# All engines in program order, weight parts ahead of the matmuls, gathers on the sync queue

## The chip, the cores and the metric

The kernel runs on one core of one Trainium2 chip. The metric is the device time in microseconds of one execution. Engines are written as in the profile: PE (TensorE, matmuls), DVE (VectorE), ACT (ScalarE), POOL (GpSimd), SP (SyncE, whose queue issues most DMAs).

## The reference

Two layers over 256 positions of width 2048, all in float32. Cut to what matters:

```python
for l in range(DEPTH):                      # 2
    h = rms_norm(x, mix_norm[l])
    proj = h @ w_in[l]                      # -> q 1024 | k 256 | v 256 | u,v 2048 | gates 4096
    q, k = apply_rope(rms_norm(q, ...)), apply_rope(rms_norm(k, ...))
    branch_a = sliding_window_attention(q, k, v, sinks[l]) @ w_attn_branch[l]   # 16 heads, window 128
    branch_b = chunked_sgu(gelu(uv), w_spatial[l], ...) @ w_sgu_branch[l]
    gates = sigmoid(gate_logits)
    merged = gates[..., :D_MODEL] * branch_a + gates[..., D_MODEL:] * branch_b
    x = x + merged @ w_out[l]
    h2 = rms_norm(x, ffn_norm[l])
    x = x + (silu(h2 @ w_gate[l]) * (h2 @ w_up[l])) @ w_down[l]                 # D_FF 5632
```

## The kernel before

**Products.** A float32 weight is split into two numbers of a shorter type, a high part `whi` (ACT copies `raw` to it, line 198) and a low part `wlo` = `raw` - `whi` (DVE, line 199). Activations are split the same way, into `uh` and `ul`. A product is three matmuls into one accumulator bank of PSUM: `whi` with `uh`, `wlo` with `uh`, `whi` with `ul` (lines 267 to 269).

**Jobs, steps, parts.** Every projection is a list of jobs, each for 1024 columns of a weight matrix (`add_job`), with four accumulator banks: two column halves c, two blocks of 128 positions t. A job runs over *units*, 512 rows of the weight with the matching transposed slice of the activations. A unit takes four *whole* steps of 12 matmuls. Each step uses one *part* of weights, 256 rows by 512 columns. In the jobs of w_out, w_gate, w_up and w_down the first unit (`M_OUT`, `M_FFN`, `M_DOWN` = 1) is done with seven products of half blocks in place of eight (`PRODUCTS`, in the order 11, t1, t2, 22, t3, 21, t4). These are seven *short* steps of 6 matmuls. Four of their weight parts are differences of others (DVE, line 193), their activations are sums too (`sums`, `sh`, `sl`), and between them ACT and DVE copy and add accumulator banks (`acc`, `p5`, `u2`, lines 294 to 317). When the last step of a column half c is done, `done(c, ...)` reads its banks: `hid`, `gate`, `xs` and so on. The half c = 0 ends one step before c = 1.

**Weights.** `raw` has four buffers of 1 MB, loaded by SP. `whi` and `wlo` have five buffers each (`W_SPLIT`).

**Transposing activations.** A finished chunk of 512 columns becomes a unit by `transposed`. Either PE transposes it (`on_pe`, line 406, eight small matmuls into `pt`), or `gathered` does. There DVE transposes 32 by 32 blocks into `blk` (line 359), of which there is one buffer, and sixteen DMAs of 32 KB, issued by POOL (line 364), carry the blocks to their places in `tt`. `done` in `transposed` splits the result `G_WAIT` = 8 steps later.

**Order.** Only PE follows the program's order. On the other engines a scheduler that estimates times places the instructions, guided by marks in the code: `tc.high_priority()` around what reads a bank, and `tc.issue_after(...)` for delayed work. Work is delayed by `after(n, fn)`, which runs `fn` n steps later, at a `tick`; a short step counts half.

The lines that set how far ahead weights are made:

```python
def next(self):
    self.load(parts[self.at][0][0] + W_LOAD)
    self.split(self.at + W_SPLIT)
    self.at += 1
```

[...]

Of the kernel before, what the change touches and what calls it, by code (L numbers as in the profile page):

```python
# [14 lines left out]
P = 128  # L15
# [17 lines left out]
W_LOAD = 4  # L33
W_SPLIT = 5
N_WARM = 8
N_BIG = 23
AHEAD = 2
G_WAIT = 8
K_TURN = 7
Q_TURN = 7  # L40
Q_FIRST = 17
Q_STEP = 4
LOAD_BY = (1, 1, 2, 2)
# [7 lines left out]
def hybrid_trunk(ctx: ExitStack, tc: tile.TileContext, x, mix_norm, w_in, q_norm, k_norm, sinks,  # L51
# [7 lines left out]
    wraw = ctx.enter_context(tc.tile_pool(name="wraw", bufs=W_LOAD))  # L59
    wsp = ctx.enter_context(tc.tile_pool(name="wsp", bufs=W_SPLIT))  # L60
# [4 lines left out]
    ps_tr = ctx.enter_context(tc.tile_pool(name="ps_tr", bufs=2, space=bass.MemoryType.PSUM))  # L65
    ps_at = ctx.enter_context(tc.tile_pool(name="ps_at", bufs=2, space=bass.MemoryType.PSUM))
# [38 lines left out]
    def add_job(cols, units=None, m=0):  # L105
# [5 lines left out]
        for i, name in enumerate(PRODUCTS if m else ()):  # L111
            for n, u in enumerate(job.units[:m]):
                a, b = held[u]
                v = {"11": (a, 0), "12": (a, 1), "21": (b, 0), "22": (b, 1)}
                src, total = {"11": ("11", None), "22": ("22", None), "21": ("21", None),
                              "t1": ("11", ("12", "11")), "t2": ("11", ("22", "11")),
                              "t3": ("12", ("22", "12")), "t4": ("11", ("21", "11"))}[name]
                parts.append((v[src], total and (v[total[0]], v[total[1]])))
                job.steps.append((name, u, n == m - 1))
        for u in job.units[m:]:  # L120
            if not job.pair:
                a = load_of(job, u)
                for h in range(2):
                    parts.append(((a, h), None))
                    job.steps.append(("whole", u, (h, 0)))
            else:
                for h in range(2):
                    a = load_of(job, u, h)
                    for c in range(2):
                        parts.append(((a, c), None))  # L130
                        job.steps.append(("whole", u, (h, c)))

    for l in range(DEPTH):
        wl = w_in[l]
        add_job([wl[:, O_KV:O_KV + CW]])
        for o in (0, O_V, O_U, O_GATE, O_GATE + CW2):
# [17 lines left out]

    class Stream:

        def __init__(self):
            self.raws, self.parts, self.lows = [], [], []
            self.at = 0

        def anchor(self):
            return self.lows[min(len(self.lows), self.at + AHEAD) - 1]

        def load(self, upto):
            while len(self.raws) < min(upto, len(loads)):
                job, srcs = loads[len(self.raws)]
                raw = wraw.tile([P, 2 * CW2], F32, tag="raw", name=nm("raw"))
                if not job.pair:
                    v = raw.rearrange("p (h k n) -> p h k n", h=2, n=CW)
                    views = [v[:, h] for h in range(2)]  # L170
                    for h in range(2):
                        src = srcs[0][:, 2 * h:2 * h + 2]
                        for k in range(2) if not self.raws else (None,):
                            ks = slice(0, 2) if k is None else slice(k, k + 1)
                            self.loaded = nc.sync.dma_start(views[h][:, ks], src[:, ks])
                else:
                    v = raw.rearrange("p (k c n) -> p k c n", c=2, n=CW)
                    views = [v[:, :, c] for c in range(2)]
                    if job.wide:
                        self.loaded = nc.sync.dma_start(raw.rearrange("p (k n) -> p k n", n=CW2), srcs[0])  # L180
                    else:
                        for c in range(2):
                            self.loaded = nc.sync.dma_start(views[c], srcs[c])
                self.raws.append(views)

        def split(self, upto):
            while len(self.parts) < min(upto, len(parts)):
                (i, j), total = parts[len(self.parts)]
                self.load(i + 1)
                raw = self.raws[i][j]  # L190
                if total is not None:
                    (ia, ja), (ib, jb) = total
                    nc.vector.tensor_tensor(out=raw, in0=self.raws[ia][ja], in1=self.raws[ib][jb], op=ALU.subtract)  # L193
                hi = wsp.tile([P, 2, CW], F32R, tag="hi", name=nm("whi"))
                lo = wsp.tile([P, 2, CW], F32R, tag="lo", name=nm("wlo"))
                one = len(self.parts) < 2
                for k in ([slice(0, 1), slice(1, 2)] if one else [slice(0, 2)]):
                    nc.scalar.activation(hi[:, k, :], raw[:, k, :], AF.Copy)  # L198
                    last = nc.vector.tensor_tensor(out=lo[:, k, :], in0=raw[:, k, :], in1=hi[:, k, :].bitcast(F32),  # L199
                                                   op=ALU.subtract)  # L200
                self.parts.append((hi, lo))
                self.lows.append(last)
# [11 lines left out]
    slot_no = [0]  # L214

# [3 lines left out]
    def tick(n=1):  # L219
        slot_no[0] += n  # L220
        due = [s for s in steps if s[0] <= slot_no[0]]
        steps[:] = [s for s in steps if s[0] > slot_no[0]]
        for _, fn in sorted(due, key=lambda s: s[0]):
            with tc.issue_after(stream.anchor().ins):
                fn()
# [3 lines left out]
    for c in range(NCH):  # L229
# [3 lines left out]
        stream.load(LOAD_BY[c])  # L233
# [26 lines left out]
    banks = [0, 1, 2, 3]  # L260
# [10 lines left out]
    def run(units, done):  # L271
# [3 lines left out]
        own = [acc(b) for b in (banks if job.pair else banks[:2])]  # L275
        if job.m:
            a, e, x, y = own
            ps = [[x, y], [e, a]]
            banks[:] = [banks[2], banks[3], banks[1], banks[0]]
            into = {"11": a, "t1": e, "t2": a, "22": e, "t3": a, "21": x, "t4": y}  # L280
            begun = {id(x), id(y)}
            held = {}
        elif job.pair:
            ps = [own[:2], own[2:]]
            begun = set()
        else:
            ps = [own]
            banks[:] = banks[2:] + banks[:2]
            begun = set()
# [6 lines left out]
        for n, (name, u, at) in enumerate(job.steps):  # L296
            hi, lo = stream.next()
            unit = units[u]
            if name != "whole":
# [5 lines left out]
                if at:  # L305
                    with tc.high_priority():
                        if name == "11":
                            nc.scalar.activation(x, a, AF.Copy)  # L308
                        elif name == "t1":
                            kept("p5", e)  # L310
                        elif name == "t2":
                            kept("u2", a)
                        elif name == "22":
                            nc.vector.tensor_tensor(out=e, in0=e, in1=held["u2"], op=ALU.add)  # L314
                        elif name == "t3":
                            nc.scalar.activation(y, a, AF.Copy)
                            nc.vector.tensor_tensor(out=a, in0=a, in1=held["p5"], op=ALU.add)
# [12 lines left out]
            if left[c] == 0:  # L330
                with tc.high_priority():
                    done(c, ps[c])
# [599 lines left out]
```

## Time and profile before

| What | Value |
|---|---|
| Median of 2 runs | 2598.59 us (2595.84 to 2601.33) |
| The profiled execution | 2600.37 us, its span 2598.7 us |
| DVE making `wlo`, 1012 instructions | 1220.3 us |
| ACT making `whi`, 1012 instructions | 1057.9 us |
| POOL issuing gathers for `tt`, 416 DMAs | 239.9 us |
| Weights moved, HBM read | 475.27 MB, 184 GB/s over the span |

The span runs from the first instruction of the program to its last. Busy time of an engine is the time in which at least one of its instructions ran; an idle time is put down to the instruction on another engine that ended it (`<-`). A row of the timeline gives the start, the duration, and in brackets the idle time before it. Consecutive matmuls overlap, so their pace is read from their starts and not from their durations.

### The profile page before, as it was taken

The page shows a single profiled execution, that of the slowest core. Times are in us where ns is not written, and L with a number is a line of the kernel's source. Part 1 is how long each engine was busy: PE and PEld are TensorE (multiplying, and loading weights), DVE is VectorE, ACT ScalarE, POOL GpSimd, SP SyncE. Part 2 cuts the span into 40 slices and gives each one's busy share as a digit, 9 for nine tenths or more (in the row PEclk, how much of TensorE's full clock was granted, in tenths as well). Part 3 has the DMA queues.
Part 4 walks back from the last instruction along what each step waited for, and adds up shares of the span by engine and source line. Part 5 has one row for each costly group of instructions (what it writes and reads, how often), then busy time and mean ns, then how long its engine had stood idle before and what let it go on. Part 6 is the DMA issues. An engine that isn't in the chain of part 4 may idle for free.

```text
span 2598.7 us, 29795 instructions
## 1 busy us (share of the span) xinstructions
PE 2515.0 (97%) x11230; PEld 2066.4 (80%) x11230; DVE 1838.5 (71%) x2109; ACT 1332.1 (51%) x1650; POOL 337.8 (13%) x559
## 2 busy tenths in 40 slices
PE   9999999999999999999989999999999999999999
PEld 7778888777788777878777788887777887788787
DVE  6785546786877687677867855467868676877786
ACT  5454444464554555455644544444645455554554
POOL 3312102030200020001123121020202000200010
PEclk9999999999999999999999999999999999999999
DMA  8645666555464655555666446564654646465654
GB/s 291 209 136 162 188 194 209 162 189 200 162 218 171 226 179 192 197 204 193 205 200 206 150 155 194 194 208 149 215 189 164 216 171 225 164 213 176 220 177 162
DMA packets 150608, 496.11 MB, mean 191 GB/s; under 512 B 16384, under 2 KB 19040, under 8 KB 150464
## 3 DMA queue, kind: packets, MB, share of 16 engines
q1 hardware_dynamic: 133408, 476.87, 54.3%
q0 software_dynamic: 16736, 17.06, 2.7%
q8 instruction: 88, 1.44, 0.2%
q14 instruction: 56, 0.46, 0.1%
q10 hardware_dynamic: 320, 0.27, 0.0%
HBM read 475.27 MB, written 2.10 MB: 184 GB/s over the span
## 4 chain that ended last, share of the span: by engine, by line
PE 89%; DVE 6%; ACT 3%; issue 1%; DMA 1%; POOL 0%; DVEq 0%; SPq 0%; ACTq 0%; POOLq 0%
PE acc L267 29%; PE acc L268 29%; PE acc L269 29%; DVE wlo L199 2%; ACT whi L198 1%; PE pt L406 1%; DVE raw L193 1%; PE po L698 1%; DVE ul L381 1%; DVE hid L878 0%; PE ppt L688 0%; ACT junk L447 0%; DMA tt<-blk 0%; DVE v L749 0%; PE psc L660 0%
## 5 line engine op out<-in xcount | busy, mean ns | idle before, releaser
L199 DVE TENSOR_TENSOR wlo<-raw,whi 128x1024 fp32r<-128x1024 f32 (+1 forms) x1012 | 1220.3, 1220 | 681.4 <-ACT whi L198 674.5
L198 ACT ACTIVATE whi<-raw 128x1024 fp32r<-128x1024 f32 (+1 forms) x1012 | 1057.9, 1057 | 1126.0 <-PE acc L269 893.2
L267 PE MATMUL acc<-whi,uh 128*128 128x512 f32 x3204 | 1260.2, 393 | 30.9 <-DVE hid L873 20.6
L268 PE MATMUL acc<-wlo,uh 128*128 128x512 f32 x3204 | 1252.3, 391 | 1.0 <-DVE wlo L199 1.0
L269 PE MATMUL acc<-whi,ul 128*128 128x512 f32 x3204 | 1252.4, 391 | 0.1
L267 PEld LDWEIGHTS acc<-whi,uh 128*128 128x128 f32 x3204 | 604.3, 189 | 162.4 <-DVE hid L873 22.2
L269 PEld LDWEIGHTS acc<-whi,ul 128*128 128x128 f32 x3204 | 604.5, 189 | 127.4 <-DVE ul L381 1.0
L268 PEld LDWEIGHTS acc<-wlo,uh 128*128 128x128 f32 x3204 | 604.6, 189 | 125.5 <-DVE wlo L199 1.9
L364 POOL DMA_DIRECT2D tt<-blk x416 | 239.9, 585 | 1868.9 <-issue 1110.4
L193 DVE TENSOR_TENSOR raw<-raw,raw 128x1024 f32<-128x1024 f32 x114 | 139.4, 1223 | 2.6
L267 PE MATMUL acc<-whi,sh 128*128 128x512 f32 x304 | 125.4, 412 | 14.1 <-ACT acc L308 14.1
L268 PE MATMUL acc<-wlo,sh 128*128 128x512 f32 x304 | 122.5, 403 | 0.0
L269 PE MATMUL acc<-whi,sl 128*128 128x512 f32 x304 | 122.0, 401 | 0.0
L267 PEld LDWEIGHTS acc<-whi,sh 128*128 128x128 f32 x304 | 60.5, 199 | 31.2 <-ACT acc L308 18.3
L269 PEld LDWEIGHTS acc<-whi,sl 128*128 128x128 f32 x304 | 59.5, 196 | 13.1
L268 PEld LDWEIGHTS acc<-wlo,sh 128*128 128x128 f32 x304 | 59.9, 197 | 12.1
L788 DVE TENSOR_TENSOR xs<-acc,xs 128x512 f32<-128x512 f32 (+1 forms) x66 | 43.8, 669 | 13.2 <-PE acc L269 13.2
L193 DVE TENSOR_TENSOR raw<-raw 128x1024 f32<-128x1024 f32 x38 | 46.5, 1225 | 1.2
L364 POOL DMA_DIRECT2D qT<-blk x64 | 37.0, 586 | 54.7 <-PE acc L269 26.2
L676 ACT ACTIVATE pr<-pr,negm 128x128 f32<-128x128 f32 (+1 forms) x64 | 28.3, 443 | 24.8 <-DVE negm L669 22.6
L872 ACT ACTIVATE hid<-acc,rhalf 128x512 f32<-128x512 f32 x44 | 28.8, 683 | 18.3 <-PE acc L269 18.3
L314 DVE TENSOR_TENSOR acc<-acc,u 128x512 f32<-128x512 f32 x38 | 26.4, 696 | 13.4 <-PE acc L269 12.0
(138 smaller groups left out, 962.0 us busy)
## 6 DMA issues: line engine op xcount, KB each, us to landing
raw<-in_w_in_dram SPq DMA_DIRECT2D x112, 1024.0 KB, 5.0
raw<-in_w_down_dram SPq DMA_DIRECT2D x88, 1024.0 KB, 6.7
raw<-in_w_gate_dram SPq DMA_DIRECT2D x80, 1024.0 KB, 5.5
raw<-in_w_up_dram SPq DMA_DIRECT2D x80, 1024.0 KB, 5.2
raw<-in_w_out_dram SPq DMA_DIRECT2D x32, 1024.0 KB, 5.5
raw<-in_w_attn_branch_dram SPq DMA_DIRECT2D x16, 1024.0 KB, 5.4
raw<-in_w_sgu_branch_dram SPq DMA_DIRECT2D x16, 1024.0 KB, 5.5
tt<-blk POOLq DMA_DIRECT2D x416, 32.0 KB, 3.6
```

What stands on the lines that cost most here:

```text
L193: nc.vector.tensor_tensor(out=raw, in0=self.raws[ia][ja], in1=self.raws[ib][jb], op=ALU.subtract)
L198: nc.scalar.activation(hi[:, k, :], raw[:, k, :], AF.Copy)
L199: last = nc.vector.tensor_tensor(out=lo[:, k, :], in0=raw[:, k, :], in1=hi[:, k, :].bitcast(F32), op=ALU.subtract)
L267: nc.tensor.matmul(ps, a, hi, start=first, stop=False, skip_group_check=True)
L268: nc.tensor.matmul(ps, a, lo, start=False, stop=False, skip_group_check=True)
L269: nc.tensor.matmul(ps, b, hi, start=False, stop=last, skip_group_check=True)
L314: nc.vector.tensor_tensor(out=e, in0=e, in1=held["u2"], op=ALU.add)
L364: nc.gpsimd.dma_start(ov[j * B:(j + 1) * B, i], blk[i * B:(i + 1) * B, j].rearrange("p k t c -> p (k t) c"))
L381: nc.vector.scalar_tensor_tensor(out=flat(unit.lo[:, kk, :]), in0=flat(src_t[:, k:k + step, :]), scalar=scaled(k0 + k), in1=flat(unit.hi[: ...
L676: nc.scalar.activation(pr4[:, h, :nk], pr4[:, h, :nk], AF.Exp, bias=nm_[:, h:h + 1], accum_out=den[:, h:h + 1])
L788: nc.vector.tensor_tensor(out=xs[:, t, sl], in0=ps[t][:, i * w:(i + 1) * w], in1=xs[:, t, sl], op=ALU.add)
L872: nc.scalar.activation(th, ps[t], AF.Tanh, scale=norm.rh[t])
```

## The change

- PE, DVE, ACT, SP and POOL all follow the order in which the program writes their instructions (`manual_schedule`). The marks for priority and issue are gone.
- Weight parts: six buffers for `whi`, five for `wlo`, and a buffer of its own (`sum`) for two of the four differences. At each step `fill` writes the low part of four steps ahead, the high part of five ahead and the difference of six ahead, and only then the step's matmuls. A load is issued once every use of the buffer's old contents stands in the program.
- A fifth accumulator bank. The two pools for transposes and attention become one of three banks.
- What DVE does on a bank in `done` is written after the next step's weight part (`soon`, `flush`). ACT's reads stay at the end of the step.
- Chains are cut up: attention's mask, exponentials, sums, transposes, values and scaling stand in steps 1, 2, 4, 6, 9 and 10 after the scores. Rotation, gelu, normalization, and the combining of a unit are spread in the same way.
- The two additions to accumulator banks in a job's short steps both stand after the seventh product.
- Gathers are issued by SP, behind and ahead of weight loads, and are split after 5 steps (`G_WAIT`), not 8. Fewer units are transposed on PE: of those of a residual, of the merge and of the hidden layer only the third, of attention none. By the two programs it is 15 units and not 28.
- In the second layer the job for q stands ahead of that for k and v.

```diff
-W_LOAD = 4
-W_SPLIT = 5
-N_BIG = 23
-AHEAD = 2
-G_WAIT = 8
+N_RAW = 4
+N_HIGH = 6
+N_LOW = 5
+N_BIG = 21
+G_WAIT = 5
...
+    wsum = ctx.enter_context(tc.tile_pool(name="wsum", bufs=1))
+    whigh = ctx.enter_context(tc.tile_pool(name="whigh", bufs=N_HIGH))
+    wlow = ctx.enter_context(tc.tile_pool(name="wlow", bufs=N_LOW))
...
-    ps_tr = ctx.enter_context(tc.tile_pool(name="ps_tr", bufs=2, space=bass.MemoryType.PSUM))
-    ps_at = ctx.enter_context(tc.tile_pool(name="ps_at", bufs=2, space=bass.MemoryType.PSUM))
+    ps_at = ctx.enter_context(tc.tile_pool(name="ps_at", bufs=3, space=bass.MemoryType.PSUM))
+    engines = mybir.EngineType
+    ctx.enter_context(tc.manual_schedule(engines={engines.PE, engines.DVE, engines.Activation, engines.SP,
+                                                  engines.Pool}))
...
+        def load(self):
+
+            while len(self.raws) < len(loads):
+                n = len(self.raws) - N_RAW
+                if n >= 0 and last_use[n] >= len(self.parts):
+                    return
+                self.fetch()
...
+        def fill(self, upto):
+            n = len(parts)
+            while True:
+                if len(self.highs) < min(upto + 1, n) and self.summed > len(self.highs):
+                    self.high()
+                elif len(self.parts) < min(upto, n) and len(self.highs) > len(self.parts):
+                    self.low()
+                elif self.summed < min(upto + 2, n):
+                    self.add()
+                else:
+                    break
+            self.load()
 
         def next(self):
-            self.load(parts[self.at][0][0] + W_LOAD)
-            self.split(self.at + W_SPLIT)
+            self.fill(self.at + min(N_LOW, 1 + self.at))
             self.at += 1
             return self.parts[self.at - 1]
...
-            banks[:] = [banks[2], banks[3], banks[1], banks[0]]
+            banks[:] = [banks[4], banks[2], banks[3], banks[1], banks[0]]
...
             hi, lo = stream.next()
+            flush()
...
-                        elif name == "22":
-                            nc.vector.tensor_tensor(out=e, in0=e, in1=held["u2"], op=ALU.add)
-                        elif name == "t3":
-                            nc.scalar.activation(y, a, AF.Copy)
-                            nc.vector.tensor_tensor(out=a, in0=a, in1=held["p5"], op=ALU.add)
+                    elif name == "t3":
+                        nc.scalar.activation(y, a, AF.Copy)
+                    elif name == "t4":
+                        nc.vector.tensor_tensor(out=e, in0=e, in1=held["u2"], op=ALU.add)
+                        nc.vector.tensor_tensor(out=a, in0=a, in1=held["p5"], op=ALU.add)
...
-                nc.gpsimd.dma_start(ov[j * B:(j + 1) * B, i],
-                                    blk[i * B:(i + 1) * B, j].rearrange("p k t c -> p (k t) c"))
+                nc.sync.dma_start(ov[j * B:(j + 1) * B, i],
+                                  blk[i * B:(i + 1) * B, j].rearrange("p k t c -> p (k t) c"))
...
-        after(G_WAIT, done)
+        if not sums:
+            after(G_WAIT, lambda: highs(0, 4, tt))
+            after(G_WAIT + 1, lambda: (lows(0, 2, tt[:, 0:2]), lows(2, 2, tt[:, 2:4]), ready()))
+            return
...
+            for n, step in ((1, masked), (2, exps), (4, inverse), (6, weights), (9, values), (10, weighted)):
+                after(n, step)
...
-                if nxt is not None:
-                    after(2, lambda: nxt.unit(o, on_pe=j == 2, sums=sums and o == 0))
-                    after(3, lambda: nxt.squares(o))
...
+                soon(lambda: added(o, ps))
+                if nxt is not None:
+                    after(1, lambda: nxt.unit(o, on_pe=o == 2, sums=sums and o == 0))
+                    after(2, lambda: nxt.squares(o))
...
-                after(2, lambda: transposed(hT, f, a, on_pe=f in fs[-2:], sums=f in fs[:M_DOWN]))
+                soon(upped)
+                after(1, lambda: transposed(hT, f, a, on_pe=f == fs[2], sums=f in fs[:M_DOWN]))
```

Two places show what moves. The first is DVE in the first round of the feed-forward part of layer 0, where the first two chunks of the hidden layer (two `hid` tiles) are finished and gathered, while the next job's short steps begin. `wlo` rows are weight parts; `blk` rows are the block transposes that open a gather. Before:

```order
L878 SCALAR_TENSOR_TENSOR hid_863_4814<-acc_870_4843,rr1_832_4612,hid_863_4814 128x512
L359 STREAM_TRANSPOSE blk_924_5143<-hid_863_4814 128x4x4x32
L199 TENSOR_TENSOR wlo_916_5103<-raw_904_5030,whi_915_5102 128x1024
L359 STREAM_TRANSPOSE blk_924_5143<-hid_863_4814 128x4x4x32
L878 SCALAR_TENSOR_TENSOR hid_866_4835<-acc_868_4841,rr0_828_4603,hid_866_4835 128x512
L199 TENSOR_TENSOR wlo_918_5121<-raw_909_5064,whi_917_5120 128x1024
L878 SCALAR_TENSOR_TENSOR hid_866_4835<-acc_867_4840,rr1_832_4612,hid_866_4835 128x512
L193 TENSOR_TENSOR raw_904_5030<-raw_909_5064,raw_904_5030 128x2x512
L199 TENSOR_TENSOR wlo_931_5170<-raw_904_5030,whi_930_5169 128x1024
```

The second gather, of `hid_866`, stands fourteen parts after the first one's block transposes. The same place now:

```order
L995 SCALAR_TENSOR_TENSOR hid_869_4852<-acc_876_4879,rr1_848_4708,hid_869_4852 128x512
L409 STREAM_TRANSPOSE blk_931_5180<-hid_869_4852 128x4x4x32 x2
L231 TENSOR_TENSOR wlo_938_5206<-raw_901_4989,whi_924_5157 128x1024
L215 TENSOR_TENSOR sum_916_5091<-raw_906_5023,raw_901_4989 128x1024
L995 SCALAR_TENSOR_TENSOR hid_872_4873<-acc_874_4877,rr0_846_4704,hid_872_4873 128x512
L995 SCALAR_TENSOR_TENSOR hid_872_4873<-acc_873_4876,rr1_848_4708,hid_872_4873 128x512
L231 TENSOR_TENSOR wlo_940_5220<-raw_906_5023,whi_937_5204 128x1024
L409 STREAM_TRANSPOSE blk_945_5233<-hid_872_4873 128x4x4x32 x2
L231 TENSOR_TENSOR wlo_947_5254<-sum_916_5091,whi_939_5218 128x1024
```

Both gathers now open within two parts, and the part for the seventh product (`wlo_947`) stands behind the second.

The second place is the queue of SP at the same point. `raw` rows are weight loads of 1 MB, the row with x16 one gather. Before:

```order
L180 DMA raw_904_5030<-in_w_gate_dram 128x2x1024
L180 DMA raw_909_5064<-in_w_gate_dram 128x2x1024
L180 DMA raw_914_5099<-in_w_gate_dram 128x2x1024
L180 DMA raw_929_5166<-in_w_gate_dram 128x2x1024
L180 DMA raw_942_5227<-in_w_gate_dram 128x2x1024
```

SP held loads alone, and the gathers stood in POOL's queue. Now:

```order
L194 DMA raw_906_5023<-in_w_gate_dram 128x2x1024
L194 DMA raw_911_5057<-in_w_gate_dram 128x2x1024
L194 DMA raw_917_5093<-in_w_gate_dram 128x2x1024
L414 DMA tt_930_5179<-blk_931_5180 32x8x32 x16
L414 DMA tt_944_5232<-blk_945_5233 32x8x32 x16
L194 DMA raw_948_5256<-in_w_gate_dram 128x2x1024
L194 DMA raw_949_5258<-in_w_gate_dram 128x2x1024
```

The load of `raw_948`, which the fifth part after the short steps needs, stands behind both gathers.

More of the change, by code (lines that the diff above doesn't have):

```diff
@@ L274, in run @@
         job_no[0] += 1
-        own = [acc(b) for b in (banks if job.pair else banks[:2])]
+        held = {}
+        begun = set()
+        n = 4 if job.pair else 2
+        own = [acc(b) for b in banks[:n]]
         if job.m:
@@ L694, in values @@
[L694 to L703 removed]
+                pss.append(pscore)
```

490 lines of the change are left out of this document (268 added, 222 removed).

## Prediction

> **What bounds the kernel now.** I read the head of the page, then the chain that ended last, then who waited on TensorE (PE), then the timeline around the longest waits.
>
> ```profile
> PE 2515.0 (97%) x11230; PEld 2066.4 (80%) x11230; DVE 1838.5 (71%) x2109; ACT 1332.1 (51%) x1650; POOL 337.8 (13%) x559
> PE 89%; DVE 6%; ACT 3%; issue 1%; DMA 1%; POOL 0%; DVEq 0%; SPq 0%; ACTq 0%; POOLq 0%
> core 0: 2598.7 us, clock 0.987
> L267 PE MATMUL acc<-whi,uh 128*128 128x512 f32 x3204 | 1260.2, 393 | 30.9 <-DVE hid L873 20.6 <-ACT acc L316 4.8 <-ACT sq L716 4.1
> L267 PE MATMUL acc<-whi,sh 128*128 128x512 f32 x304 | 125.4, 412 | 14.1 <-ACT acc L308 14.1
> 999.83 0.39 PE L268 MATMUL acc<-wlo,uh 128*128 128x512 f32 x1
> ...
> 1019.09 0.39 PE L269 MATMUL acc<-whi,ul 128*128 128x512 f32 x1
> 1019.32 1.03 PE L406 MATMUL pt<-ident,hid 128*128 128x128 f32 x8
> 1020.11 0.48 PE L267 MATMUL acc<-whi,uh 128*128 128x512 f32 x1
> 1020.43 0.40 PE L268 MATMUL acc<-wlo,uh 128*128 128x512 f32 x1
> ```
>
> PE carries 89% of the chain. Between 999.83 and 1019.09 stand 85 intervals, so a large matmul takes 0.2266 us. There are 3 x (3204 + 304) = 10524 of them: 2384.7 us that the change doesn't touch. Only the 214 us beside them can move: small matmuls, waits and a slow clock. The waits of PE:
>
> ```profile
> PE acc L267 <- DVE hid L873: 20.6, 4, 5.1
> PE pt L406 <- DVE ul L381: 17.3, 9, 6.6
> PE acc L267 <- ACT acc L308: 14.1, 10, 2.1
> PE po L698 <- DVE pr L663: 9.7, 8, 2.0
> PE acc L267 <- ACT acc L316: 4.8, 4, 1.5
> PE acc L267 <- ACT sq L716: 4.1, 2, 2.0
> PE pt L406 <- ACT p L294: 2.6, 1, 2.6
> PE pt L406 <- DVE gate L851: 2.2, 4, 0.9
> ```
>
> They sum to 75.4 us: accumulator banks not yet read out, transposes that want a bank, attention scores not yet masked. A wait costs more than itself:
>
> ```profile
> 619.57 0.50 PE L267 MATMUL acc<-whi,sh 128*128 128x512 f32 x1 [2.12 <-ACT acc L308]
> ...
> 621.01 0.63 PE L269 MATMUL acc<-whi,sl 128*128 128x512 f32 x1
> 621.43 0.63 PE L267 MATMUL acc<-whi,sh 128*128 128x512 f32 x1
> ...
> 708.84 0.79 PE L267 MATMUL acc<-whi,uh 128*128 128x512 f32 x1 [5.14 <-DVE hid L873]
> 709.43 0.63 PE L268 MATMUL acc<-wlo,uh 128*128 128x512 f32 x1
> 709.86 0.63 PE L269 MATMUL acc<-whi,ul 128*128 128x512 f32 x1
> ...
> 712.83 0.40 PE L267 MATMUL acc<-whi,sh 128*128 128x512 f32 x1
> ```
>
> After the wait of 5.14 us nine matmuls start 0.43 us apart, not 0.23: 9 x 0.2 = 1.8 us more. A wait of 2.12 us was followed by the same. The mean clock of 0.987 bounds this loss at 1.3% of the span, 33.8 us; the four waits of 5.1 us and the one of 6.6 alone are 5 x 1.8 = 9. I take 24 us, some 13 waits of 2 us or more (not every one of them shows it).
>
> [...]
>
> **The change part by part.** A whole step is 12 matmuls, 2.72 us; one of the seven short steps that open a job of w_out, w_gate, w_up or w_down is 6, 1.36 us. Let t = 0 be the start of the short steps.
>
> *Waits removed.* The fifth bank lets product 11 open a job in a bank that nobody reads, so the banks of the previous job have 1.4 us more or longer; reading them out stands in front of later work of the same step. Masking, exponentials and sums stand in steps of their own, so PE's attention work finds them done. In the second layer q goes before k and v, so that the last unit is wanted later. I take all 75.4 us and all 24 us of slow clock off, and put back below what the new order brings.
>
> *Transposes on PE.* 13 of 28 units (104 transposes) leave PE for the gather. One unit delays the second matmul behind it from 1019.09 + 0.45 to 1020.43: 0.89 us. 13 x 0.89 = 11.6 us off. DVE and ACT do as many passes over these tiles as before but for 26 more block transposes, 18 us on an engine at 71%, beside PE.
>
> *Gathers from SP.* This is the large term. blk is one buffer. The next pair of block transposes may write it only when all sixteen DMAs of the gather before have landed. Before, DVE's second pair stood behind fourteen more parts. Now it stands one step later, and DVE, in program order, makes nothing while it waits. Nine times the two gathers fall around the seven short steps: after the first w_out job of each layer, after the first w_up job in each of the three rounds of each layer, and once in the last w_down of layer 0.
>
> ```profile
> 617.57 3.49 DVE L199 TENSOR_TENSOR wlo<-raw,whi 128x1024 fp32r<-128x1024 f32 x3
> L193 DVE TENSOR_TENSOR raw<-raw,raw 128x1024 f32<-128x1024 f32 x114 | 139.4, 1223 | 2.6
> 686.93 1.30 DVE L359 STREAM_TRANSPOSE blk<-hid 128x512 f32<-128x512 f32 x2
> 661.25 0.71 DVE L878 SCALAR_TENSOR_TENSOR hid<-acc,rr,hid 128x512 f32<-128x512 f32 x1
> 1.72 1.87 SPq L175 DMA_DIRECT2D raw<-in_w_in_dram  x4
> out_dram<-xs SPq DMA_DIRECT2D x2, 128.0 KB, 1.9
> L364 POOL DMA_DIRECT2D tt<-blk x416 | 239.9, 585 | 1868.9 <-issue 1110.4 <-DVE blk L359 315.0 <-ACT whi L198 259.8
> raw<-in_w_gate_dram SPq DMA_DIRECT2D x80, 1024.0 KB, 5.5
> ```
>
> DVE: a part 1.16 us (3.49 / 3), a sum as much, a pair of hid 1.33, of block transposes 1.30. Five low halves are held, so DVE can't run further ahead: at t = -2.72 it makes part 3, the first hid pair and the transposes, and is done at 1.1. Then part 4, a sum, the second hid pair, part 5: done at 5.9. SP has no gather before; its nearest rows are loads, four in 1.87 us, so 0.45 us each, landing 1.9 us for its smallest. Sixteen of them from 1.2 end landing at 1.2 + 15 x 0.45 + 1.9 = 9.9. DVE waits 4 us, transposes until 11.2, and has part 6 at 12.3. PE wants it at 6 x 1.36 = 8.16: a wait of 4.2 us, and 1.8 us of slow clock behind it. The sum for the second half's banks, four parts later at 17.7, is then in time (PE is there at 18.3). 9 x 6.0 = 54 us. Bounds: nothing if sixteen land by 5.9, 0.2 us each, which no SP row comes near; with POOL's 0.585 us each 10.1 us, since the loads queued behind the second gather also come late: they leave at 11.3 + 16 x 0.45 = 18.6, land 5.5 us later, and their first part is ready at 26.4, just when PE gets there. At 0.585 us they are 2.1 us late. I take 0.45, from SP's own rows.
>
> The other gathers are three steps or more from each other, or followed by whole steps, where five parts ahead are 10.9 us of cover. If that goes, the next late thing is a weight load behind sixteen issues (7.2 us); it has some 10 us.
>
> *What the new order puts into short steps*, an estimate of 24 us in all:
>
> ```profile
> 571.63 0.64 ACT L447 ACTIVATE junk<-xs 128x512 f32<-128x512 f32 x1
> 572.15 0.21 ACT L447 ACTIVATION_READ_ACCUMULATOR junk<-xs 128x1 f32 x1
> L872 ACT ACTIVATE hid<-acc,rhalf 128x512 f32<-128x512 f32 x44 | 28.8, 683 | 18.3 <-PE acc L269 18.3
> ```
>
> Squares of xs, 1.7 us a pair, stand twice between ACT's copies of the banks, which in these steps have under 1 us to spare: 4 us for the job after w_out in each layer, 8. A unit on PE at the head of the steps, with DVE owing block transposes and low halves as well: 8 over six jobs. The tanh pair (1.3 us) ahead of the copies in ten w_up jobs: 0.4 each, 4. Attention's remainder: 4.
>
> *At nothing:* the sums of weights and the additions to banks are as many as before; starting loads are the same and bound by DMA; POOL only loses work.
>
> Sum: 2598.7 - 75.4 - 24 - 11.6 + 54 + 24 = 2565.7 us of span. The profiled execution's time was 2600.4 and the median of the runs shown 2598.6, so I take 2566 as the median.
>
> **The rivals.** *The gathers land in time.* A gather's piece is 32 KB, an eighth of SP's smallest load, and could issue or land faster than any row shows. Then the 54 us fall: 2512.
>
> *SP is slow with gathers, and the kernel is slower.* [...] At 0.585 us a piece gains and losses cancel (9 x 10.1 = 91: 2603); beyond, both the sixth part and the loads behind slip: at 0.7 us 8 + 1.8 + 3.9 = 13.7 a pair, 123 in all: 2635. For it: POOL's row; against it: SP's issues.
>
> [...]
>
> *DVE in program order becomes the bound in attention.*
>
> ```profile
> 120.00:275.00 155.00, 147.72 (x739) 120.75 (x738) 110.54 (x204) 79.62 (x149) 34.52 (x53) 0.98 0.48 153
> ```
>
> DVE is busy 110.5 of 155 us there, and the order now has steps with a part, a normalization and masked scores together, more than PE's step is long. Banks of u and v are then read late. Should PE's waits there (pr 9.7 and sq 4.1 us) come back and double, it is 2566 + 28 = 2594, no change. Against it: five parts are held ahead, and a fifth bank.
>
> **How the numbers follow.** Forecast, with its own range of 2545 to 2590: 0.48. Gathers in time: 0.24. SP slow: 0.12. DVE in attention, or waits that merely move: 0.16. 2% of the time, 52 us, is about what a measurement of this kernel tells from no change. Faster than 2546 are the second case and the lowest part of the first: 0.31. Slower than 2650 is the far end of SP's: 0.08. The rest, 0.61, is within 2%. The range reaches from the second case's 2512 past the point of balance, 2603: 2510 to 2612.
>
> **What would show it.** Right: the waits on hid, L308, pr and sq gone; DVE's block transposes waiting on DMA some 4 us at nine places, each followed by a wait of PE of about 4 us on a wlo that is the seventh part, and by slow matmuls; SP's sixteen issues in about 7 us. Wrong: no DVE wait on blk (2512), waits of ACT on raw behind gathers (2600 and more), or PE waiting in attention on sq and pr. I would be wrong most if SP's rate for small pieces is not that of its loads.

## The result, and the profile after

| | Median | Range | Ratio to before (95%) |
|---|---|---|---|
| before | 2598.59 us | 2595.84 to 2601.33 | |
| changed | 2674.73 us | 2670.94 to 2678.51 | 1.0293 (1.0215 to 1.0371) |

The change makes the kernel 2.9% slower. 2566 us were forecast, with a range that ended at 2612. The profiled execution's span is 2669.2 us, 103.5 us over the sum of the forecast (2565.7).

The rows of the changed kernel that answer to those of before. From the page, the engines' busy time and the chain that ended last by engine:

```profile
PE 2531.8 (95%) x11126; PEld 2057.3 (77%) x11126; DVE 1851.9 (69%) x2135; ACT 1318.5 (49%) x1628; POOL 47.5 (2%) x47
PE 73%; SPq 11%; DMA 6%; DVE 5%; issue 2%; ACT 1%; POOL 0%; DVEq 0%; ACTq 0%; POOLq 0%
```

The core's granted clock is 0.981, where it was 0.987.

Of the waits of PE (for what; us in total, times, longest):

```profile
PE acc L321 <- DVE wlo L231: 68.9, 30, 6.9
PE acc L320 <- ACT whi L223: 32.9, 16, 4.2
PE acc L320 <- ACT p L345: 7.1, 10, 0.8
PE acc L320 <- ACT u L345: 5.0, 5, 1.0
PE acc L320 <- ACT acc L365: 2.9, 5, 0.6
PE ppt L767 <- DVE pr L743: 0.3, 1, 0.3
```

The chain tells it at once: SP's queue, which had no share of 1% before, carries 11%. The waits of before are gone as forecast (hid 20.6, bank copies 14.1, masked scores 9.7 to 0.3 us). In their place PE waits 101.8 us for parts of weights. Before, its wait on wlo was 1.0 us in all.

The timeline at one of the nine places where two gathers fall around short steps, by engine: DVE, then ACT, then SP, then PE.

```profile
955.05 1.31 DVE L409 STREAM_TRANSPOSE blk<-hid 128x512 f32<-128x512 f32 x2 [7.33 <-DMA tt<-blk]
956.28 1.18 DVE L231 TENSOR_TENSOR wlo<-sum,whi 128x1024 fp32r<-128x1024 f32 x1
973.60 2.36 DVE L231 TENSOR_TENSOR wlo<-raw,whi 128x1024 fp32r<-128x1024 f32 x2 [10.39 <-ACT whi L223]
972.51 2.00 ACT L223 ACTIVATE whi<-raw 128x1024 fp32r<-128x1024 f32 x2 [20.82 <-DMA raw<-in_w_gate_dram]
943.06 24.16 SPq L414 DMA_DIRECT2D tt<-blk  x32
967.32 2.47 SPq L194 DMA_DIRECT2D raw<-in_w_gate_dram  x4
957.52 0.80 PE L321 MATMUL acc<-wlo,uh 128*128 128x512 f32 x1 [5.87 <-DVE wlo L231]
958.12 0.63 PE L322 MATMUL acc<-whi,ul 128*128 128x512 f32 x1
...
961.53 0.59 PE L321 MATMUL acc<-wlo,uh 128*128 128x512 f32 x1
961.96 0.40 PE L322 MATMUL acc<-whi,ul 128*128 128x512 f32 x1
973.62 0.50 PE L320 MATMUL acc<-whi,uh 128*128 128x512 f32 x1 [1.73 <-ACT whi L223]
974.88 0.50 PE L321 MATMUL acc<-wlo,uh 128*128 128x512 f32 x1 [0.76 <-DVE wlo L231]
...
975.74 0.63 PE L321 MATMUL acc<-wlo,uh 128*128 128x512 f32 x1
976.16 0.63 PE L322 MATMUL acc<-whi,ul 128*128 128x512 f32 x1
```

The gather costs twice. First DVE stands 7.33 us before its second pair of block transposes, since the sixteen DMAs of the first gather still read `blk`; PE waits 5.87 us for the part behind it, and nine matmuls run at half pace (0.43 us from start to start). Then SP lets four weight loads go only at 967.32. Its 32 pieces stand in one row of 24.16 us, but some 3 us of that are a wait between the two gathers: the second one can start only when DVE's second transposes end, at 956.36, and its own sixteen pieces then hold the loads back by 10.8 us. ACT stands 20.82 us for the first of them, and PE waits once more, 1.73 and 0.76 us, again with slow matmuls. Measured by the starts of its matmuls against 0.2266 us each, PE loses 10.5 to 13.3 us at each of the nine places, 108 us in all. Some 14 us of these are short waits on `p`, `u` and a bank copy in the same steps, which have nothing to do with gathers; 94 are left.

The same second wait stands at six places with a single gather, where DVE doesn't wait for `blk`. PE's row on `whi` counts 16 waits: one at the start, nine, and these six. One of them:

```profile
790.41 0.50 PE L320 MATMUL acc<-whi,uh 128*128 128x512 f32 x1 [3.11 <-ACT whi L223]
789.30 2.00 ACT L223 ACTIVATE whi<-raw 128x1024 fp32r<-128x1024 f32 x2 [14.59 <-DMA raw<-in_w_down_dram]
```

The first wait stands at two more places, where the merge's gathers open, once in each layer (8.67 and 8.09 us of DVE on `blk`, 3.10 and 2.51 us of PE). In layer 0, DVE and PE:

```profile
414.88 1.30 DVE L409 STREAM_TRANSPOSE blk<-gate 128x512 f32<-128x512 f32 x2 [8.67 <-DMA tt<-blk]
416.11 4.59 DVE L231 TENSOR_TENSOR wlo<-raw,whi 128x1024 fp32r<-128x1024 f32 x4
417.34 0.50 PE L321 MATMUL acc<-wlo,uh 128*128 128x512 f32 x1 [3.10 <-DVE wlo L231]
```

### The profile page after: what moved, and what is told of

Read it like the earlier page. It is cut to its first block, busy times and chain, and to the rows that moved or that the text cites. A ratio compares the mean times of both kernels' runs of the same rounds, so it can differ in the third digit from the quotient of the medians.

```text
span 2669.2 us, 30413 instructions
## 1 busy us (share of the span) xinstructions
PE 2531.8 (95%) x11126; PEld 2057.3 (77%) x11126; DVE 1851.9 (69%) x2135; ACT 1318.5 (49%) x1628; POOL 47.5 (2%) x47
## 4 chain that ended last, share of the span: by engine, by line
PE 73%; SPq 11%; DMA 6%; DVE 5%; issue 2%; ACT 1%; POOL 0%; DVEq 0%; ACTq 0%; POOLq 0%
PE acc L321 24%; PE acc L320 24%; PE acc L322 23%; SPq L414 11%; DVE wlo L231 2%; DMA raw<-in_w_down_dram 1%; DMA raw<-in_w_attn_branch_dram 1%; DMA raw<-in_w_out_dram 1%; DMA raw<-in_w_gate_dram 1%; DVE blk L409 1%; DMA tt<-blk 1%; ACT whi L223 1%; PE po L778 1%; PE psc L736 1%; DVE hid L995 0%
## 5 line engine op out<-in xcount | busy, mean ns | idle before, releaser
L231 DVE TENSOR_TENSOR wlo<-raw,whi 128x1024 fp32r<-128x1024 f32 (+1 forms) x936 | 1123.1, 1219 | 638.3 <-PE acc L321 364.5
L223 ACT ACTIVATE whi<-raw 128x1024 fp32r<-128x1024 f32 (+1 forms) x936 | 972.7, 1057 | 1065.6 <-PE acc L322 690.8
L321 PE MATMUL acc<-wlo,uh 128*128 128x512 f32 x3204 | 1266.7, 395 | 68.9 <-DVE wlo L231 68.9
L320 PE MATMUL acc<-whi,uh 128*128 128x512 f32 x3204 | 1272.0, 397 | 45.0 <-ACT whi L223 32.9
L223 ACT ACTIVATE whi<-sum 128x1024 fp32r<-128x1024 f32 x76 | 80.7, 1062 | 98.7 <-DVE sum L215 51.2
L231 DVE TENSOR_TENSOR wlo<-sum,whi 128x1024 fp32r<-128x1024 f32 x76 | 92.4, 1216 | 7.4 <-PE acc L321 6.8
L409 DVE STREAM_TRANSPOSE blk<-hid 128x512 f32<-128x512 f32 x32 | 20.8, 688 | 45.9 <-DMA tt<-blk 45.9
L896 DVE TENSOR_TENSOR xs<-acc,xs 128x512 f32<-128x512 f32 (+1 forms) x66 | 41.3, 667 | 10.4 <-PE acc L322 10.4
L215 DVE TENSOR_TENSOR raw<-raw,sum 128x1024 f32<-128x1024 f32 x38 | 46.5, 1224 | 2.2 <-DMA raw<-in_w_up_dram 0.9
L215 DVE TENSOR_TENSOR sum<-raw 128x1024 f32<-128x1024 f32 x38 | 46.3, 1220 | 0.7 <-DMA raw<-in_w_up_dram 0.7
L215 DVE TENSOR_TENSOR raw<-raw,raw 128x1024 f32<-128x1024 f32 x38 | 46.3, 1220 | 0.0
L215 DVE TENSOR_TENSOR sum<-raw,raw 128x1024 f32<-128x1024 f32 x38 | 46.3, 1218 | 0.0
```

The costliest lines, as they stand in the source:

```text
L215: nc.vector.tensor_tensor(out=self.raw(dst), in0=self.raw(total[0]), in1=self.raw(total[1]), op=ALU.subtract)
L320: nc.tensor.matmul(ps, a, hi, start=first, stop=False, skip_group_check=True)
L321: nc.tensor.matmul(ps, a, lo, start=False, stop=False, skip_group_check=True)
L409: nc.vector.transpose(blk[:, :, :, t, :].rearrange("p j k c -> p k j c"), src[:, t, :].rearrange("p (k j c) -> p k j c", j=4, c=B))
L896: nc.vector.tensor_tensor(out=xs[:, t, sl], in0=ps[t][:, i * w:(i + 1) * w], in1=xs[:, t, sl], op=ALU.add)
```

## The experiments

The theory after these rows: what costs is the time in which SP issues sixteen pieces, once through `blk` and once through the loads behind. The rival: the new order of the steps is what costs, and PE would wait elsewhere if the gathers were free. Every run was timed beside runs of the kernel before, whose medians were 2595.7 to 2599.1 us.

### Four runs on the gathers

```diff
two_blk:
-        blk = turned.tile([P, 4, 4, NT, B], F32, tag="blk", name=nm("blk"))
+        blk = turned.tile([P, 4, 4, NT, B], F32, tag="blk", name=nm("blk"), bufs=2)
pool:
-                nc.sync.dma_start(ov[j * B:(j + 1) * B, i],
+                nc.gpsimd.dma_start(ov[j * B:(j + 1) * B, i],
before_sp (in the kernel before):
-                nc.gpsimd.dma_start(ov[j * B:(j + 1) * B, i],
+                nc.sync.dma_start(ov[j * B:(j + 1) * B, i],
```

The run pool_two has both of the first two edits. Where there are two buffers, `N_BIG` is 20 and not 21.

> The changed kernel with two buffers for blk (and one general 4 KB buffer less). Theory (SP's sixteen pieces take 10.4 us, which costs twice: DVE waits for blk, and the loads queued behind are late): the first cost goes, some 68 us at the nine pairs of gathers; the second gather starts about 3 us earlier, so the loads behind it are less late, some 20 us more: 2580, and 2600 if the loads gain nothing. The waits of PE on whi behind late loads stay at the other six gathers. Rival (the new order of the steps, not the gathers, is what costs): DVE's wait on blk goes, but PE waits elsewhere instead: 2640 or more.

> The changed kernel with the gathers issued by POOL, as before, and one blk. Theory: the loads no longer stand behind gathers, which takes off the late loads, some 40 us at the nine pairs and 35 at other gathers; DVE still waits for blk, at POOL's 0.585 us a piece a little less long: about 2585. ACT's long waits on raw go, DVE's on blk stay at 4 to 6 us. Rival (the order costs): 2640 or more.

> Both: gathers issued by POOL and two buffers for blk. Theory: both costs go, 68 and 75 us: 2525, below the kernel before by some 70. Rival: with the gathers off the path the new order of the steps still costs what it put into them: 2580 to 2620.

> The kernel before with its gathers issued by SP and nothing else. Theory (SP's queue alone makes loads late by some 4 us behind a gather, at fifteen or so of the 26 gathers): 2640 to 2660. Rival (the SP queue is harmless as long as DVE doesn't wait for blk, which stands fourteen parts apart here): 2600.

PE's waits are in us in total, the clock is the mean that was granted.

| Run | Median | Ratio to before | PE on wlo | PE on whi | clock |
|---|---|---|---|---|---|
| changed | 2674.7 | 1.0293 (1.0215 to 1.0371) | 68.9 | 32.9 | 0.981 |
| two_blk | 2645.2 | 1.0176 (1.0160 to 1.0191) | 11.9 | 77.5 | 0.979 |
| pool | 2629.3 | 1.0115 (1.0100 to 1.0130) | 72.3 | 1.7 | 0.982 |
| pool_two | 2547.3 | 0.9802 (0.9788 to 0.9817) | 5.4 | 1.4 | 0.996 |
| before_sp | 2588.5 | 0.9958 (0.9944 to 0.9972) | 0.8 | none | 0.991 |

Each edit alone gives 30 and 45 us, a third and a half of what was expected (95 and 90); both together give 127. The two costs stand one behind the other on the same path, and the wait that is taken away uncovers the other. The timeline of two_blk, SP, ACT and PE at the same place:

```profile
935.50 21.93 SPq L414 DMA_DIRECT2D tt<-blk  x32
957.52 2.39 SPq L194 DMA_DIRECT2D raw<-in_w_gate_dram  x4
962.73 2.00 ACT L223 ACTIVATE whi<-raw 128x1024 fp32r<-128x1024 f32 x2 [18.59 <-DMA raw<-in_w_gate_dram]
963.84 0.79 PE L320 MATMUL acc<-whi,uh 128*128 128x512 f32 x1 [7.70 <-ACT whi L223]
```

DVE doesn't wait for `blk`, but SP still needs 21.93 us for the two gathers. PE arrives earlier at the parts of the load and waits 7.70 us where it waited 1.73. In pool the loads are in time, and DVE's wait has become longer. POOL at this place, and PE:

```profile
927.11 6.33 POOL L414 DMA_DIRECT2D tt<-blk  x11 [154.61 <-ACT whi L223]
933.81 0.58 POOL L414 DMA_DIRECT2D tt<-blk  x1 [0.37 <-DMA tt<-blk]
936.54 2.31 POOL L414 DMA_DIRECT2D tt<-blk  x4 [2.14 <-issue]
942.65 0.79 PE L321 MATMUL acc<-wlo,uh 128*128 128x512 f32 x1 [7.53 <-DVE wlo L231]
```

POOL issues a piece each 0.575 us (6.33 / 11), but stops after eleven, since the twelfth waits 0.37 us for an earlier one to land, and takes from 927.11 to 938.85 for sixteen. So the rival is refuted for the bulk: with the gathers off both paths the written order is 2% faster than the kernel before.

before_sp was expected to lose 40 to 60 us, and gains 10. The piece is as slow there, as SP's timeline in the kernel before with this one edit shows:

```profile
654.38 10.41 SPq L364 DMA_DIRECT2D tt<-blk  x16
664.89 2.56 SPq L180 DMA_DIRECT2D raw<-in_w_gate_dram  x4
668.30 16.07 SPq L364 DMA_DIRECT2D tt<-blk  x16
```

16 pieces take 10.41 us, 0.651 each. (The second gather takes 16.07; it stands right behind four loads. More on this in the last section.) But four loads stand between the two gathers, and DVE has no wait on `blk` there (3.1 us in two waits over the whole run). So the slow queue alone is not what costs; it is where the gathers stand, ahead of loads and of parts that are due. The run changes more than the queue, though: in the kernel before the scheduler places DVE's work, and with this edit it put the second gather of such a pair eight parts behind the first, where it had been thirteen or fourteen. PE's waits on hid and ul fall by it (20.6 to 7.3 and 17.3 to 10.1 us), those on the bank copies rise (14.1 to 25.5). How much of the gain of 10 us this makes was not followed.

### Half the pieces, the distance, the fifth bank, the squares

```diff
split (one blk):
-                nc.sync.dma_start(ov[j * B:(j + 1) * B, i],
+                (nc.sync if i < 2 else nc.gpsimd).dma_start(ov[j * B:(j + 1) * B, i],
sp_late (one blk, gathers by SP):
-                    after(1, lambda: nxt.unit(o, ...
+                    after(4 if o % 2 else 1, lambda: nxt.unit(o, ...
-                after(1, lambda: transposed(hT, f, a, ...
+                after(4 if f % 2 else 1, lambda: transposed(hT, f, a, ...
pt_four (pool_two with):
-    banks = [0, 1, 2, 3, 4]
+    banks = [0, 1, 2, 3]
-            banks[:] = [banks[4], banks[2], banks[3], banks[1], banks[0]]
+            banks[:] = [banks[2], banks[3], banks[1], banks[0]]
pt_spread (pool_two with):
-                    after(2, lambda: nxt.squares(o))
+                    after(6, lambda: nxt.squares(o))
-                        after(4, lambda: nxt.finish())
+                        after(9, lambda: nxt.finish())
-                    after(1, lambda: nxt.unit(o, on_pe=o == 2, ...
+                    after(2 if o == 2 else 1, lambda: nxt.unit(o, on_pe=o == 2, ...
-                after(1, lambda: transposed(hT, f, a, on_pe=f == fs[2], ...
+                after(2 if f == fs[2] else 1, lambda: transposed(hT, f, a, on_pe=f == fs[2], ...
```

> The changed kernel with one blk, where SP issues eight of a gather's sixteen pieces and POOL the other eight. It halves the time that a gather holds SP (10.4 to 5.2 us). Theory (the time to issue sixteen pieces is what decides, twice): DVE waits for blk until the pieces of both queues have landed, some 9 us after the first, and PE some 4 us at nine places, with slow matmuls 6; the loads are no longer late, at pairs or single gathers: 2547 + 9 x 5 = 2590, 2575 to 2605. Rival (a gather costs by its presence, whoever issues it): 2629, as by POOL alone.

split: 2545.9 us (2545.3 to 2547.1), 0.9800 (0.9784 to 0.9815). With half the pieces on another queue, and nothing else changed, 129 of the 2674.7 us are gone, as many as with POOL and two buffers, and more than expected. The timeline, DVE, POOL, SP and PE:

```profile
915.07 1.30 DVE L409 STREAM_TRANSPOSE blk<-hid 128x512 f32<-128x512 f32 x2 [2.94 <-DMA tt<-blk]
908.02 4.61 POOL L414 DMA_DIRECT2D tt<-blk  x8 [161.18 <-ACT whi L223]
922.29 2.44 SPq L194 DMA_DIRECT2D raw<-in_w_gate_dram  x4
917.54 0.50 PE L321 MATMUL acc<-wlo,uh 128*128 128x512 f32 x1 [1.51 <-DVE wlo L231]
```

DVE still waits, 2.94 us, PE 1.51, and no slow matmuls follow (0.23 us from start to start). The loads leave at 922.29 and are in time: over the whole run PE waits 1.7 us on whi, once, and 12.6 on wlo. SP has eight pieces of each gather to issue where it had sixteen: its row of both gathers begins at 907.47 and is 14.72 us long, where it was 24.16, the wait between the gathers included. Here that is worth 129 us.

> The changed kernel, gathers by SP and one blk, but of each pair the second gather opens after the next job's seven short steps and not one step behind the first (residual and hidden layer). Theory: DVE no longer waits for blk, and four loads stand between the two gathers, so the twelve us a pair fall to what a single gather costs, 0 to 5 us: about 2590, 2560 to 2620. Rival (it is the slow SP queue itself that costs, wherever the gathers stand): 2640 or more.

sp_late: 2581.9 us, 0.9937 (0.9921 to 0.9952), as expected. SP issues all pieces at its old pace, but with loads between two gathers:

```profile
932.19 2.53 SPq L194 DMA_DIRECT2D raw<-in_w_gate_dram  x4
941.02 10.40 SPq L414 DMA_DIRECT2D tt<-blk  x16
```

PE's waits on wlo fall to 10.2 us and on whi to 6.3. Others come (13.9 us on hid, 9.3 on xs), so it stays 36 us behind split. Distance alone, with SP as slow as it was, thus does most of what half the pieces on another queue do: 93 of 129 us.

> Gathers by POOL and two buffers for blk, with four accumulator banks in turn and not five. Theory (the fifth bank is what removed the waits of 20.6 us on hid and 14.1 on acc): about 35 us of waits and 10 of slow clock come back, 2590. Rival (the written order alone reads the banks early enough): 2550.

pt_four: 2575.4 us, 0.9909 (0.9893 to 0.9925), 28 us over pool_two. Who waits, by the waits of PE:

```profile
PE acc L320 <- ACT acc L359: 33.1, 28, 1.8
PE acc L320 <- DVE hid L986: 3.9, 4, 1.4
```

Without the fifth bank PE waits 28 times for the copy of product 11 (line 359), 33.1 us where it was 14.1 before: the written order alone makes this wait longer, and the bank removes it. The waits on hid of 20.6 us do not come back, so the written order removed those.

> Gathers by POOL and two buffers for blk as in the run of 2547 us, and besides: the squares of xs six steps after the sum, not two (the norm's end nine, not four), and the unit that PE transposes two steps after, not one. Theory (what the new order puts into the short steps is a cost of its own): PE's waits on u and on acc L365 (4.6 and 3.0 us) and on xs and hid at pt (5.8 and 4.5) go, with some of the slow clock behind them: 2527. Rival (these waits only move to the next late thing): 2545.

pt_spread: 2537.1 us, 0.9766 (0.9749 to 0.9784), 10 us faster than pool_two, half of what was expected. The waits on acc L365 and on xs and hid at pt are gone; that on u fell to 2.5 us, but that on p rose from 9.9 to 13.9, and 4.8 us on xs at a large matmul are new. Part of the gain only moved.

### Transposes, differences, and the best of them

```diff
pt_onpe (pool_two with):
+ on_pe=j == 2 (residual, merge), on_pe=f in fs[-2:] (hidden layer), on_pe=c == 1 (attention)
best_c (changed kernel with split, two buffers for blk, and):
-                    after(2, lambda: nxt.squares(o))
+                    after(6, lambda: nxt.squares(o))
-                        after(4, lambda: nxt.finish())
+                        after(9, lambda: nxt.finish())
best_b (best_c with), best_a (pt_spread with):
-                elif self.summed < min(upto + 2, n):
+                elif self.summed < min(upto + 3, n):
best_d (best_c with):
+        def lead(self):
+            total = parts[self.summed][1] if self.summed < len(parts) else None
+            return 2 if total and isinstance(total[1][0], str) else 3
...
-                elif self.summed < min(upto + 2, n):
+                elif self.summed < min(upto + self.lead(), n):
```

> Gathers by POOL and two buffers for blk (the run of 2547 us), with the units that the kernel before transposed on PE back on PE: 28 and not 15. Theory (a unit on PE is worth 0.89 us): 13 x 0.89 = 11.6 us, 2559. Rival (with a pair gathered from the second half of a job, the gathers hold up units, so that PE's transposes are cheaper here): 2547 or less; or more than 2565, if PE also waits for DVE's sums ahead of the transposes.

pt_onpe: 2562.3 us, 0.9867 (0.9852 to 0.9881), 15 us over pool_two by the medians, 6 to 16 by the ends of the two ranges. The term of 11.6 us lies within this. But PE's waits on ul at its transposes, 10.2 us, come back with the units, and other waits get shorter (all of PE's waits are 52.6 us against 48.8), so what the transposes cost by themselves is not separated.

> The run of 2537 us (gathers by POOL, two buffers for blk, squares and PE's units later), with the differences of weights one step earlier: seven steps ahead, not six. Theory (ACT's copy of the bank to p stands behind a high part that waits for DVE's difference, 13.9 us in 17 waits): most of these waits go, 2525. Rival (DVE and ACT are only late elsewhere): 2537.

> The changed kernel with each gather's pieces issued half by SP and half by POOL, two buffers for blk, squares six steps later and the differences one step earlier; PE's units as in the changed kernel. Theory: the rest of DVE's wait on blk (32.5 us in all with one buffer) and PE's 12.6 us on wlo behind it go, squares and differences as in the runs beside: 2525. Rival (two gathers that hold SP for 5 us each, now close together, make the loads late): 2540 or more.

> The changed kernel with each gather's pieces issued half by SP and half by POOL, two buffers for blk, and the squares six steps after the sum: the run of 2527 us without the earlier differences. Theory (PE's waits on p come from differences that DVE makes late, and these alone are left in): waits on p of some 10 us come back, 2536. Rival (the earlier differences gave nothing): 2526 or less.

> The same with the differences one step earlier, but for the second one, which overwrites a buffer whose low part is still wanted: it stays where it was. Theory: the waits on p go again, 2526. Rival (the second difference is the late one, and holds the high parts as before): 2536.

| Run | Median | Ratio to before | PE on p | PE on acc L367 |
|---|---|---|---|---|
| best_a | 2545.1 | 0.9806 (0.9791 to 0.9820) | none | 8.1 |
| best_b | 2526.6 | 0.9729 (0.9713 to 0.9745) | none | 7.7 |
| best_c | 2519.8 | 0.9700 (0.9686 to 0.9715) | 6.8 | 3.1 |
| best_d | 2525.5 | 0.9724 (0.9708 to 0.9740) | none | 7.7 |

In best_a and best_b the difference for the third product is written into its buffer one part before the low part of product 11 has been read from it, so that part is computed from other numbers. best_d leaves this one in its place and computes all as before. Two theories fell here. The earlier differences do take away the waits on p, but the additions to banks (line 367, shifted by four lines in best_d) and PE's transposes are then later by as much or more: best_d is 5.7 us slower than best_c by the medians. And two gathers by halves with two buffers do not make loads late: in best_c PE waits on whi once, 1.4 us.

best_c is faster than both kernels, by 3.0% than before. What is left in it, by the waits of PE (its clock is 0.997 of a span of 2518.1 us):

```profile
PE pt L472 <- DVE xs L896: 7.9, 5, 2.7
PE acc L320 <- ACT p L345: 6.8, 10, 0.8
PE acc L321 <- DVE wlo L231: 3.4, 4, 2.6
PE acc L320 <- DVE acc L367: 3.1, 6, 1.0
```

The rows on u and acc L365 (5.0 and 2.9 us in the changed kernel) are gone with the later squares. On blk DVE no longer waits.

## Why the prediction was wrong, point by point

**What the gathers cost: the term of 54 us.** This is what failed, and the prediction had named the reason as the one that would make it most wrong: SP's rate for small pieces is not that of its loads. The gathers cost some 130 us and not 54. By best_c against the changed kernel, PE's waits on wlo and whi are 101.8 us against 4.8, and the clock's loss (the span times what the granted clock lacks) is 50.7 us (2669.2 x 0.019) against 7.6: 97 + 43 = 140 us. split, which changes nothing but the queue of half the pieces, takes 129 off. Three steps of the working were wrong.

- "I take 0.45, from SP's own rows." The mechanism, the nine places and their order on DVE came as the prediction put them. The rate did not: 0.65 us a piece (10.41 / 16), slower than POOL's, where the prediction chose the row of the same queue with 1 MB loads. The end of the sixteen came 3 us later, and DVE waited 7.33 us, not 4. Then the loads behind the second gather, whose first part was to be ready "just when PE gets there", were late as well. The rival that SP is slow had worked this out: 10.1 us a pair at 0.585 and 13.7 at 0.7, so 12.2 at 0.652, 110 us for nine. Measured were 94. It was given 0.12.
- "If that goes, the next late thing is a weight load behind sixteen issues (7.2 us); it has some 10 us." Sixteen issues are 10.4 us, and the margin is gone with single gathers too. At six of these PE waits 2.7 to 4.0 us, 19.2 in all.
- "The other gathers are three steps or more from each other, or followed by whole steps, where five parts ahead are 10.9 us of cover." At the merge's gathers that cover was not enough: DVE stands 8.67 and 8.09 us for `blk`, and PE waits 3.1 and 2.5 for the part behind. With the slow matmuls behind four of the six (behind the merge's two waits the pace is full, 0.23 us) these six and two places make some 35 us that no case of the prediction had in its sum.

So 54 became 129 by place (94 + 35), or 140 by the two rows. That leaves 18 to 28 of the 103.5 us between forecast and measurement, which lie in the terms below.

**The rest of the sum.** Without the 54 us it comes to 2512. The runs in which the gathers hold up little are at 2546 (split) and 2547 (pool_two), some 35 us above. In pool_two PE's waits are 48.8 us. The sum had left in place 3.8 us of small waits of the kernel before and put 24 back, so some 21 of the 35 are waits that it didn't have; the rest was not traced.

**Waits removed, 75.4 us.** Right. The rows are gone, and three of the causes were told apart: the bank copies went by the fifth bank (28 us in pt_four), hid by the order, and the wait on ul by having fewer units on PE, for it comes back with them in pt_onpe (10.2 of 17.3 us).

**The slow clock, 24 us.** Right once nothing waits long: 33.8 us before, 7.6 in best_c, 26 less. In the changed kernel the waits behind gathers brought back more than that (the loss is 50.7 us there). The length of a wait alone did not tell whether slow matmuls followed: after 1.73 and 0.76 us, one matmul apart, matmuls ran at half pace (975.74 to 976.16 above, 0.42 us), while after 1.51 us in split and 3.10 us at the merge in layer 0 the pace stayed full (0.23 us from start to start).

**Transposes, 11.6 us.** It agrees with pt_onpe, 6 to 16 us, in which the waits on ul are included.

**What the order puts into short steps, 24 us.** The places were right, the sum too low. In the changed kernel p, u, the copies and the gates stand with 7.1 + 5.0 + 2.9 + 4.4 us among PE's waits, and line 367 and the transposes of hid, gate and xs with 3.1 + 2.8 + 2.0 + 1.2: 28.5 us. In pool_two, where PE is held up less by gathers, more shows: 45 (48.8 less 3.8). Of the 28.5 the squares are 7.9 us (u and acc L365), against the 8 that were set down for them.

**Rivals.** "The gathers land in time", 2512: not so, and where they hold nothing up (pool_two) the kernel is at 2547; best_c, which has the squares later as well, is at 2520. "DVE in attention becomes the bound": no; masked scores 9.7 us before, 0.3 after. "SP is slow with gathers, and the kernel is slower": this is what happened, to its far end and beyond, since it too left the single gathers and the merge's at nothing.

## What to carry to other kernels

- A price for an operation on a queue that has never carried it is not the price of that queue's other work. Where two rows bound it, and the sum turns sign between them, the chance of the bad side is not a tail: here SP's loads gave 0.45 us, POOL's pieces 0.585, and the truth, 0.65, lay outside both.
- SP's queue, with small pieces ahead of large loads, delayed the loads by the pieces' whole issue time (10.4 us a gather), and DVE, in program order, turned a buffer's wait (7.33 us) into one of everything behind it (5.87 us of PE). Count both, for each place, against the time at which the next load is due.
- When two waits lie in series, removing one shows little (30 and 45 us here) and removing both shows it all (127). Before dropping a theory on a small gain, remove the second wait as well.

## What the runs showed of the hardware that was not expected

How long a 32 KB piece took from issue to landing grew with loads in flight beside it. By the view of the gathers' line (min, median, max) it was 1.9 us in the median from SP in the changed kernel, 4.9 from POOL in pool, and 2.0 over both queues in split:

```profile
DMA to landing us min/median/max: 1.9/1.9/8.1
DMA to landing us min/median/max: 1.8/4.9/7.8
DMA to landing us min/median/max: 1.8/2.0/6.6
```

In the kernel before, POOL's pieces that left from 663.25 up to the first of four loads (issued from 667.18 on) took 1.8 to 1.9 us, and those that left beside the loads, up to 672, 5.1 to 6.2. On SP's own queue it was longer. In before_sp the gather at 668.30 stands right behind four loads, issued from 664.89 on, and its first four pieces took 8.2 to 9.7 us. At the place above in the changed kernel little of this shows: 29 of the 32 pieces took 1.9 to 2.0 us, the others at most 3.0. That view in before_sp, for the window 668 to 671:

```profile
DMA to landing us min/median/max: 8.2/8.9/9.7
```

Issued by SP the same pieces are many more packets than issued by POOL. The rows of the page for SP's queue (q1) and POOL's (q0) (packets, MB, share of 16 engines), of the changed kernel:

```profile
q1 hardware_dynamic: 329248, 500.51, 56.2%
q0 software_dynamic: 352, 0.25, 0.2%
```

Of pool:

```profile
q1 hardware_dynamic: 133408, 476.87, 54.2%
q0 software_dynamic: 23392, 23.89, 3.5%
```

Of 720 pieces, SP's are 195840 packets, 272 each, and POOL's 23040, 32 each. Whether this is why SP takes 0.65 us to issue one was not tried.
